# Layer A attention: the preparation of the first output rows held step by step, and 14 gate products moved to the last twelve steps

## The chip, the cores and the metric

The kernel runs on one core of one Trainium2 chip, as a single program. The metric is the device time of one execution in microseconds. A core has five engines with instruction queues of their own: TensorE (PE; its weight loads are PEld), VectorE (DVE), ScalarE (ACT), GpSimd (POOL) and SyncE (SP), which here issues all DMAs. Every queue is worked off in the order in which the program stands; an instruction that waits for a semaphore holds what is queued behind it on its engine.

## The reference, cut to what matters

A decoder of two layers over 2048 positions and 1024 channels, in float32. Only the first layer (A) is touched by the change:

```python
u = rmsnorm(h, norm_a_g[i])
proj = u @ w_in_a[i]
q, k, v, f_logit, gate = jnp.split(proj, [...], axis=-1)
...
o = fox_attention(q, k, v, log_f).reshape(b, s, WIDTH_A)
h = h + (o * jax.nn.silu(gate)) @ w_out_a[i]
```

`fox_attention` is causal softmax attention with 16 heads of 64 channels and a bias from a running sum of forget gates. What matters here are the last two factors: the attention's output `o` is divided by its row sums, multiplied by the SiLU of the gate, and projected with `w_out_a`.

## The kernel before, in words

A float32 product of full precision is made of three products: every operand is split into a high part (rounded to fp32r) and the remainder, and high x high, high x low and low x high are added up in PSUM.

`layer_a` projects q, k, v and the forget logits, runs `attention_a`, and then `out_a`, the output projection. The attention's loop (L1171) has 320 steps: 16 heads, in each four chunks of 512 queries, and for the chunks 2, 4, 6 and 8 steps of two key blocks (20 a head). A step does the following.

- `scores` (L997): up to four products (L1013, L1014) into two `sc` banks; ScalarE takes the exponential into an `st` tile (L1029) and rounds it to `ph` (L1032); **GpSimd subtracts, `pl` = `st` - `ph` (L1033, "the split" below)**; VectorE adds to the row sums (L1042).
- `values` (L1047), three steps later (`V_LAG`): for each key block one product with `ph` and one with `pl` (L1057).
- `ahead`: the maxima of score rows for a later chunk (L968 on TensorE, L976 and L981 on VectorE), whose row is written into the key operand by four small DMAs (L578). These end some steps before the loop does, since no further head follows.
- `feed` (L1155): products of the gate projection (L1099) as filler. There are 768: four chunks of 512 columns, eight row tiles, eight depth tiles, three products each. In step n the filler is brought to (768 - `KEPT`)(n + 1)/320, so 2.25 products a step; `KEPT` = 48 are left for the tail behind the loop. Every 12 products need new gate weights (`wr`, two buffers, 512 KB from DRAM, L1076). Where a chunk of columns begins anew, sixteen operand tiles of 256 KB are loaded as well (L1085). A finished bank of 24 products goes through VectorE and ScalarE (L1110 to L1112) and is stored as `gt` (L1113).

The output projection needs, for each pair of heads and chunk, a prepared operand: main and correction part of the attention's output added, times the reciprocals `rd`, times the gate `gt`, split in high and low (`gated`, L1231: L1240, L1241, L1244, ScalarE's L1245, L1246). The four inputs are loaded by `gated_load` (L1221 to L1226: `om`, `oc`, `gt` and twice `rd`). The first two pairs are prepared inside the attention's loop, on GpSimd: their loads and all five instructions are written in steps 284 and 298 (`PREP_AT`). The third pair's loads are written behind the loop (L1203), and its first add belongs to the projection's first step. The tiles `qn` that take `om` and `gt` have two buffers, so that a pair's loads wait until the pair before has done with them.

The order on an engine is not that of the source: a scheduler takes instructions by their place in the program and by when it believes them ready, and may put a later instruction ahead. `keep_in_program_order` holds an instruction back until those before it in the program have been placed.

Of the kernel before, what the change touches and what calls it, by code (L numbers as in the profile page):

```python
# [13 lines left out]
F32R = mybir.dt.float32r  # L14
# [4 lines left out]
ALU = mybir.AluOpType  # L19
# [4 lines left out]
P = 128  # L24
# [8 lines left out]
CH = 512  # L33
# [10 lines left out]
LOAD_AT = 7  # L44

PREP_AT = (284, 298)

RAW_AT = 302

KEPT = 2 * 3 * NDT  # L50

PAIRS_LOADED = 5
PAIRS_READY = 2
# [47 lines left out]
def f_(ap):  # L101
    return ap.bitcast(F32)


class Pairs:
# [13 lines left out]
    def prepare(self, s, engine=None, pin=False):  # L119
        if s % 4 == 0:  # L120
            self.Y[s // 4] = self.t.sb("big", [P, 4, 2, CH], F32R)
        self.t.gated(self.y(s), self.tiles.pop(s), engine or self.t.nc.vector, pin)
        self.ready = s + 1

    def y(self, s):
        return self.Y[s // 4][:, s % 4]
# [27 lines left out]
class Trunk:  # L154
# [727 lines left out]
    def attention_a(self, op):  # L882


        nc, tc, d = self.nc, self.tc, self.d
# [17 lines left out]
        steps = [(u, p) for u, (h, ch) in enumerate(units) for p in range(2 * ch + 2)]  # L903
# [248 lines left out]
        filler, fed, total = gate(), 0, NCH * NDT * NDT * 3  # L1152
# [18 lines left out]
        for n, (u, p) in enumerate(steps):  # L1171
            h, ch = units[u]
            if n % per_head == LOAD_AT and h + 1 < H:
                more_pieces(len(pieces) + 1)
            target = per * (n + AHEAD + 1) // per_head + 1
            ahead(target - 1)
            ends = len(pending) == V_LAG and closes(pending[0])
            if ends:
                values(pending.pop(0))
            pending.append(scores(n, u, p))  # L1180
            ahead(target)
            if len(pending) > V_LAG and not ends:
                values(pending.pop(0))
            if p == 2 * ch + 1:
                if h == H - 1 and ch in (0, NCH - 1):
                    due.append((n + SUM_LAG, (h, ch and 1, ch + 1)))
                elif ch == NCH - 1 and h == H - 2:
                    due.append((n + SUM_LAG, (h,)))
                elif ch == NCH - 1 and h % 2:
                    due.append((n + SUM_LAG, (h - 1, 0, NCH, 2)))  # L1190
            while due and due[0][0] <= n:
                recips(*due.pop(0)[1])
            if n == 0:
                self.ps("mx", [P, 512])
            feed((total - KEPT) * (n + 1) // len(steps), pause=True)
            if n == RAW_AT:
                raw = self.sb("big", [P, NDT // 2, D])
                for p in range(NDT // 2):
                    op.weight_load(p, raw[:, p])
            if n in PREP_AT:  # L1200
                op.load(PREP_AT.index(n), ("qn", "wh", "qn", "wl"))
                op.prepare(PREP_AT.index(n), nc.gpsimd)
        op.load(2, ("qn", "wh", "qn", "wl"))  # L1203
        gate_bank, weight_slots = "mx", cycle(["st", "wr"])
        for item in pending:
# [11 lines left out]
    def gated_load(self, ch, p, tiles):  # L1217
        nc, d = self.nc, self.d
        rows, cols = slice(p * P, (p + 1) * P), slice(ch * CH, (ch + 1) * CH)
        m, c, g, rb = tiles  # L1220
        nc.sync.dma_start(out=m, in_=d["om"][rows, cols])  # L1221
        nc.sync.dma_start(out=c, in_=d["oc"][rows, cols])
        nc.sync.dma_start(out=g, in_=d["gt"][rows, cols])
        for s in range(2):
            h = 2 * p + s
            nc.sync.dma_start(  # L1226
                out=rb[s * HD : (s + 1) * HD, :],
                in_=d["rd"][h : h + 1, cols].to_broadcast([HD, CH]),
            )

    def gated(self, y, tiles, engine, pin=False):  # L1231

# [455 lines left out]
```

## Time and profile before

| what | us |
|---|---|
| timed runs, median of 3 (lowest, highest) | 2422.66 (2418.39, 2423.58) |
| profiled execution | 2421.78 |
| its span | 2420.0 |
| TensorE busy (share of the span) | 2402.8 (99%) |
| GpSimd busy (share of the span) | 994.6 (41%) |

A row of the timeline gives the start in us, the duration in us, the engine, the source line, the operation and its tiles (out<-in), the shapes, the number of instructions merged, and in brackets the idle time ahead with what ended it. Rows marked SPq are the issue of a DMA, not its transfer. The attention's loop lies between about 596 us (first split) and 1432 us (last split), the tail of gate products ends at 1444 us, and the output projection follows. Numbers behind PE are busy time and, in brackets, the count of instructions. The duration of a TensorE product is modelled and overlaps the next; its pace is read from the distance of starts.

### The profile page before, as it was taken

What the parts mean: (1) busy time and instruction counts of PE and PEld (TensorE: products, weight loads), DVE (VectorE), ACT (ScalarE), POOL (GpSimd) and SP (SyncE); (2) the same over time, 40 slices, a digit from 0 to 9 for tenths busy, and PEclk for the clock granted to TensorE, in tenths of its full rate; (3) what the DMA queues carried; (4) which work ended last, traced back from release to release, by engine and by line L of the source; (5) the groups of instructions that cost most, each with busy time, mean ns of one, the idle gap of its engine ahead of it and who ended that gap; (6) DMA issues with size and microseconds to landing.
All of it is one profiled execution on the core that took longest, in us unless ns stands there. A gap on an engine that the chain in (4) does not pass through costs nothing.

```text
span 2420.0 us, 36279 instructions
## 1 busy us (share of the span) xinstructions
PE 2402.8 (99%) x11960; PEld 2026.4 (84%) x11960; DVE 1732.2 (72%) x4086; ACT 1262.2 (52%) x2504; POOL 994.6 (41%) x642
## 2 busy tenths in 40 slices
PE   9999999999999999999999999999999999999999
PEld 7888899988888888888888888888888888888887
DVE  7656567735898888888888866456766633677775
ACT  5433324323878778877877761135423322466664
POOL 0000000011877777777778862200011000378885
PEclk9999999999999999999999999999999999999999
DMA  6656555677654655566466549975434574765552
GB/s 192 201 170 193 152 154 167 197 229 233 186 165 128 198 165 151 149 207 175 132 178 181 178 134 304 304 248 164 131 92 122 160 253 144 236 213 181 182 183 75
DMA packets 356989, 436.04 MB, mean 180 GB/s; under 512 B 65280, under 2 KB 248608, under 8 KB 350624
## 3 DMA queue, kind: packets, MB, share of 16 engines
q1 hardware_dynamic: 356800, 433.71, 59.3%
q8 instruction: 95, 1.56, 0.3%
q14 instruction: 94, 0.77, 0.1%
HBM read 273.69 MB, written 159.79 MB: 179 GB/s over the span
## 4 chain that ended last, share of the span: by engine, by line
PE 92%; DMA 5%; DVE 1%; ACT 1%; issue 0%; POOL 0%; SPq 0%; ACTq 0%; POOLq 0%; DVEq 0%
PE b L790 31%; PE pa L1057 10%; PE pb L1099 7%; PE pb L1515 7%; PE sc L1013 5%; PE sc L1014 5%; PE mx L968 5%; PE b L1286 4%; PE b L752 4%; PE b L1369 2%; PE pa L1454 2%; PE pb L752 2%; DMA wr<-wg 1%; PE fl L359 1%; PE pa L359 1%; PE pb L359 1%
## 5 line engine op out<-in xcount | busy, mean ns | idle before, releaser
L790 PE MATMUL b<-wh,big 128*128 128x512 f32 (+3 forms) x2560 | 772.2, 374 | 1.1 <-ACT wh L502 0.9
L1033 POOL TENSOR_TENSOR big<-st,big 128x1024 fp32r<-128x1024 f32 (+1 forms) x320 | 656.2, 2071 | 239.2 <-ACT big L1032 158.9
L790 PEld LDWEIGHTS b<-wh,big 128*128 128x128 f32 x2560 | 470.6, 188 | 72.4 <-ACT wh L502 2.8
L790 PE MATMUL b<-wl,big 128*128 128x512 f32 (+3 forms) x1280 | 473.8, 370 | 0.8 <-DVE wl L503 0.7
L1042 DVE TENSOR_TENSOR ac<-ac,st 128x512 f32<-128x512 f32 (+3 forms) x576 | 352.6, 612 | 51.9 <-ACT st L1029 27.2
L1029 ACT ACTIVATE st<-sc 128x512 f32<-128x512 f32 (+1 forms) x512 | 273.6, 583 | 117.5 <-PE sc L1023 48.2
L1057 PE MATMUL pa<-big 128*128 128x512 f32 (+3 forms) x1280 | 318.9, 365 | 0.7 <-POOL big L1033 0.7
L1032 ACT CAST big<-st 128x1024 fp32r<-128x1024 f32 (+1 forms) x320 | 295.3, 923 | 8.5
L790 PEld LDWEIGHTS b<-wl,big 128*128 128x128 f32 x1280 | 241.3, 189 | 37.2 <-DVE wl L503 5.2
L1057 PEld LDWEIGHTS pa<-big 128*128 128x128 f32 x1280 | 229.0, 190 | 39.0 <-POOL big L1033 2.4
L981 DVE TENSOR_REDUCE mt<-mx 128x1 f32<-128x384 f32 (+1 forms) x360 | 214.3, 598 | 30.7 <-PE mx L968 28.2
L1013 PE MATMUL sc<-big 128*128 128x512 f32 (+3 forms) x640 | 232.9, 368 | 0.1
L511 ACT ACTIVATE sq<-b,r 128x512 f32<-128x512 f32 (+2 forms) x128 | 77.8, 608 | 295.4 <-PE b L790 295.4
L1014 PE MATMUL sc<-big 67*128 67x512 f32 (+3 forms) x640 | 229.6, 367 | 0.0
L968 PE MATMUL mx<-big 66*128 66x512 f32 (+2 forms) x600 | 224.9, 380 | 0.2
L1099 PE MATMUL pb<-wh,wr 128*128 128x512 f32 x488 | 177.4, 396 | 5.5 <-DMA wr<-wg 5.3
L513 DVE TENSOR_REDUCE sm<-sq 128x8 f32<-128x512 f32 (+2 forms) x128 | 74.8, 584 | 138.0 <-ACT sq L511 137.8
L892 POOL MEMSET rot<- 128x512 bf16 x1 | 0.5, 525 | 418.3 <-PE pb L359 418.3
L1417 POOL TENSOR_TENSOR big<-big,tri 128x1024 fp32r<-128x1024 f32 x60 | 144.3, 2405 | 59.9 <-DVE big L1414 59.9
L976 DVE CUSTOM_DVE_ANT_0 mx<-mx,rot 128x384 f32<-128x384 f32 (+2 forms) x240 | 146.8, 617 | 17.9 <-PE mx L968 17.3
L1013 PEld LDWEIGHTS sc<-big 128*128 128x128 f32 x640 | 121.7, 190 | 21.7 <-DVE st L560 0.5
L1014 PEld LDWEIGHTS sc<-big 67*128 67x128 f32 x640 | 121.8, 190 | 19.3
(285 smaller groups left out, 4124.0 us busy)
## 6 DMA issues: line engine op xcount, KB each, us to landing
wr<-wg SPq DMA_DIRECT2D x62, 512.0 KB, 4.2
va<-st SPq DMA_DIRECT2D x32, 512.0 KB, 4.7
ka<-st SPq DMA_DIRECT2D x64, 256.0 KB, 3.8
ut<-big SPq DMA_DIRECT2D x16, 1024.0 KB, 7.0
big<-ka SPq DMA_DIRECT2D x16, 1024.0 KB
big<-qa SPq DMA_DIRECT2D x16, 1024.0 KB, 7.8
qb<-st SPq DMA_DIRECT2D x64, 256.0 KB, 3.7
big<-qb SPq DMA_DIRECT2D x16, 1024.0 KB, 7.7
```

The lines of the kernel that those rows point to most:

```text
L790: nc.tensor.matmul(ps[:, :n], u[tb // 4][:, dt, us], W[k][dt], start=(dt == 0 and i == 0), stop=(dt == NDT - 1 and i == 2),)
L968: mm = nc.tensor.matmul(ps, qb[:66, i * P : (i + 1) * P], kb[:66, k0:k1], start=True, stop=True,)
L981: nc.vector.reduce_max(o, ps, axis=AX.X)
L1013: nc.tensor.matmul(o, ka[:, ks], qa[:, qs], start=not (last and n_), stop=False)
L1014: nc.tensor.matmul(o, kb[:, ks], qb[:, qs], start=False, stop=not diag)
L1029: nc.scalar.activation(pf[:, off : off + w], ps[:, :w], AF.Exp, scale=HD**-0.5)
L1032: nc.scalar.copy(ph[:, :tw], pf[:, :tw])
L1033: nc.gpsimd.tensor_tensor(pl[:, :tw], pf[:, :tw], f_(ph[:, :tw]), ALU.subtract)
L1042: nc.vector.tensor_tensor(a_, a_, pf[:, off : off + w], ALU.add)
L1057: nc.tensor.matmul(pv[:, q0 : q0 + w], v[:, k, :], src[:, off : off + w], start=(p == 0 and n_ == 0 and i == 0), stop=(last and n_ == 1 an ...
L1099: nc.tensor.matmul(ps, w[:, dt // 2 % 2, wk, dt % 2, :], us[dt][uk], start=(dt == 0 and i == 0), stop=(dt == NDT - 1 and i == 2),)
L1515: nc.tensor.matmul(ps, yt(i, y, slice(p, p + 1))[:, 0, :], W[nh][p // 4][:, k, p % 4, :], start=(p == 0 and n_ == 0), stop=(p == NDT - 1 a ...
```

## The change

Two things. First, the preparation of the two pairs becomes a generator, `gated_parts`. Its loads are written in steps 284 and 298 as before; the instructions follow from five steps later on (`PREP_LAG`), one a step: the add, two multiplications, a step with nothing, ScalarE's copy, the subtraction. Each is kept in program order. Second, `DENSE` = 14 gate products are taken out of the even spread and added in the last twelve steps (`DENSE_STEPS`): the filler now stands at 706(n + 1)/320, and from step 308 on 14/12 more with every step.

```diff
 PREP_AT = (284, 298)
+PREP_LAG = 5
...
 KEPT = 2 * 3 * NDT
+DENSE = 14
+DENSE_STEPS = 12
...
+    def prepare_parts(self, s):
+        if s % 4 == 0:
+            self.Y[s // 4] = self.t.sb("big", [P, 4, 2, CH], F32R)
+        self.ready = s + 1
+        return self.t.gated_parts(self.y(s), self.tiles.pop(s))
...
-            feed((total - KEPT) * (n + 1) // len(steps), pause=True)
+            ahead_of = DENSE * max(0, n + 1 + DENSE_STEPS - len(steps)) // DENSE_STEPS
+            feed((total - KEPT - DENSE) * (n + 1) // len(steps) + ahead_of, pause=True)
...
             if n in PREP_AT:
-                op.load(PREP_AT.index(n), ("qn", "wh", "qn", "wl"))
-                op.prepare(PREP_AT.index(n), nc.gpsimd)
+                s = PREP_AT.index(n)
+                op.load(s, ("qn", "wh", "qn", "wl"))
+                prepared = op.prepare_parts(s)
+            if any(0 <= n - at - PREP_LAG < 6 for at in PREP_AT):
+                next(prepared, None)
...
+    def gated_parts(self, y, tiles):
+        nc, pin = self.nc, self.tc.keep_in_program_order
+        m, c, g, rb = tiles
+        yh, yl = (y[:, k] for k in range(2))
+        yield pin(nc.gpsimd.tensor_tensor(m, m, c, ALU.add))
+        yield pin(nc.gpsimd.tensor_tensor(m, m, rb, ALU.mult))
+        yield pin(nc.gpsimd.tensor_tensor(m, m, g, ALU.mult))
+        yield
+        yield pin(nc.scalar.copy(yh, m))
+        yield pin(nc.gpsimd.tensor_tensor(yl, m, f_(yh), ALU.subtract))
```

What moves on the engines is seen in the order of the built programs. In the changed kernel the lines of the attention's loop have numbers higher by 9 (the split L1033 is L1042 there, a gate product L1108, a load of `wr` L1085), those of `gated_load` by 13, and those from `gated` on by 24; its pieces of the preparation are L1248, L1249, L1250, ScalarE's L1252, and L1253.

GpSimd, before, from step 273 (head 13) on: `big<-st,big` is a split, `qn<-qn,wh` the first add of a pair, `qn<-qn,wl` and `qn<-qn` its multiplications, `big<-qn,big` its last subtraction. The scheduler has put the preparation eleven steps ahead of the place where it is written.

```order
L1033 TENSOR_TENSOR big<-st,big 128x1024
L1240 TENSOR_TENSOR qn<-qn,wh 128x512
L1241 TENSOR_TENSOR qn<-qn,wl 128x512
L1244 TENSOR_TENSOR qn<-qn 128x512
L1033 TENSOR_TENSOR big<-st,big 128x1024 x3
L1240 TENSOR_TENSOR qn<-qn,wh 128x512
L1033 TENSOR_TENSOR big<-st,big 128x1024
L1241 TENSOR_TENSOR qn<-qn,wl 128x512
```

In the changed program the first pair stands in the second half of head 14, and the second in the last head, with the first add of the third pair (L1264) between; these are the rows from step 302 on:

```order
L1042 TENSOR_TENSOR big<-st,big 128x1024 x2
L1248 TENSOR_TENSOR qn<-qn,wh 128x512
L1042 TENSOR_TENSOR big<-st,big 128x896
L1249 TENSOR_TENSOR qn<-qn,wl 128x512
L1042 TENSOR_TENSOR big<-st,big 128x384
L1250 TENSOR_TENSOR qn<-qn 128x512
L1042 TENSOR_TENSOR big<-st,big 128x1024
L1264 TENSOR_TENSOR qn<-qn,wh 128x512
L1042 TENSOR_TENSOR big<-st,big 128x1024 x2
L1253 TENSOR_TENSOR big<-qn,big 128x512
```

In before only splits stand in the last head's rows on GpSimd. Now five instructions of the preparation stand between its first eight splits, one behind each of several splits.

SyncE, before, ahead of the two gate weights (`wr<-wg`) that step 292 and the next need. `big<-m` is a row of maxima, `om<-sq`, `oc<-sq` and `gt<-sq` are stores of results, and the last two rows are loads for the second and third pair:

```order
L578 DMA big<-m 1x128x1 x8
L1067 DMA om<-sq 64x512
L1113 DMA gt<-sq 128x512
L1068 DMA oc<-sq 64x512
L1076 DMA wr<-wg 128x1024 x2
L1223 DMA qn<-gt 128x512
L1221 DMA qn<-om 128x512
```

The same place in the changed program:

```order
L587 DMA big<-m 1x128x1 x8
L1076 DMA om<-sq 64x512
L1077 DMA oc<-sq 64x512
L1085 DMA wr<-wg 128x1024 x2
L1235 DMA wh<-oc 128x512
L1239 DMA wl<-rd 64x512 x2
L1234 DMA qn<-om 128x512
L587 DMA big<-m 1x128x1 x4
```

The store of a gate tile no longer stands ahead of the two loads of `wr`, and behind them come the second pair's loads, which in before stood some twenty steps earlier.

TensorE, before, from the last products of step 319 with an earlier split (`pa<-big`) on, through its gate products (`pb<-wh,wr`, `pb<-wl,wr`) and the products of the last three splits to the first gate product of the tail (`mx<-wh,st`):

```order
L1057 MATMUL pa<-big 128x512 x4
L1099 MATMUL pb<-wh,wr 128x512
L1099 MATMUL pb<-wl,wr 128x512
L1099 MATMUL pb<-wh,wr 128x512
L1057 MATMUL pa<-big 128x512 x6
L1057 MATMUL pa<-big 128x384 x2
L1057 MATMUL pa<-big 128x256 x2
L1057 MATMUL pa<-big 128x128 x2
L1099 MATMUL mx<-wh,st 128x512
```

The same place in the changed program:

```order
L1066 MATMUL pa<-big 128x512 x4
L1108 MATMUL pb<-wl,wr 128x512
L1108 MATMUL pb<-wh,wr 128x512 x2
L1108 MATMUL pb<-wl,wr 128x512
L1108 MATMUL pb<-wh,wr 128x512
L1066 MATMUL pa<-big 128x512 x6
L1066 MATMUL pa<-big 128x384 x2
L1066 MATMUL pa<-big 128x256 x2
L1066 MATMUL pa<-big 128x128
L1108 MATMUL mx<-wh,st 128x512
```

Three gate products stand in the last step in before, five now, and each of the steps ahead of it has about one more. The tail behind the loop holds 48 in both; the very last product with a split now stands behind 16 of them instead of ahead of all.

## Prediction

> **What bounds the kernel now.** I read the page first, then the windows of 50 us over the whole attention stage, then TensorE's waits, and last the timeline of SyncE, GpSimd and TensorE at the places where a window of TensorE is not full. The page's first part says that TensorE is busy for nearly all of the span:
>
> ```profile
> PE 2402.8 (99%) x11960; PEld 2026.4 (84%) x11960; DVE 1732.2 (72%) x4086; ACT 1262.2 (52%) x2504; POOL 994.6 (41%) x642
> ```
>
> So only what TensorE waits for can be gained, and only what makes it wait can be lost. The waits of the attention's products (L1057, L1099) stand in these rows of the view of waits (whole run: total us, times, longest):
>
> ```profile
> PE pb L1099 <- DMA wr<-wg: 5.3, 5, 1.5
> ...
> PE b L1286 <- DVE big L1297: 0.7, 1, 0.7
> PE pa L1057 <- POOL big L1033: 0.7, 2, 0.4
> ```
>
> The first is a gate product (L1099) that waits for its gate weights `wr`; the last is an output product (L1057) that waits for the low half that GpSimd makes (L1033); the middle one lies in the projection behind the attention. The windows (TensorE's busy time is the first figure behind the length) put the gate waits at the three changes of the gate's chunk, and once more at 1358 us:
>
> ```profile
> 800.00:850.00 50.00, 48.61 (x238) 39.94 (x237) 43.90 (x98) 39.20 (x62) 38.16 (x19) 1.00 0.74 221
> 1000.00:1050.00 50.00, 48.51 (x241) 40.12 (x240) 41.62 (x95) 38.05 (x62) 37.49 (x19) 1.00 0.63 185
> 1200.00:1250.00 50.00, 49.43 (x242) 40.78 (x241) 42.89 (x96) 40.51 (x64) 38.68 (x20) 1.00 0.47 121
> 1250.00:1300.00 50.00, 49.19 (x242) 40.68 (x240) 43.88 (x100) 38.60 (x63) 36.34 (x19) 1.00 0.71 219
> 1300.00:1350.00 50.00, 50.00 (x249) 41.81 (x248) 43.79 (x98) 38.58 (x62) 46.67 (x26) 1.00 0.68 190
> 1350.00:1400.00 50.00, 48.66 (x238) 39.55 (x237) 42.93 (x96) 38.27 (x62) 41.03 (x22) 1.00 0.47 148
> 1400.00:1450.00 50.00, 49.71 (x230) 40.37 (x231) 32.34 (x47) 33.41 (x51) 31.25 (x15) 1.00 0.44 135
> ```
>
> Row by row TensorE lacks 1.39, 1.49, 0.57, 0.81, 0, 1.34 and 0.29 us: 5.9 us, or 0.24% of the span. The window 1300 to 1350 holds most of the old preparation, with GpSimd at 46.67 of 50 us, and TensorE lacks nothing in it. That sets the scale of what can be won. The granted clock is 1.00 in every row.
>
> **The preparation, moved and held.** The view of its tiles gives the first and the last instruction of each preparation on GpSimd, with the shortest, median and longest time in ns and the first and last start:
>
> ```profile
> L1240 POOL TENSOR_TENSOR qn<-qn,wh x3: 1286/1290/1304, 1309.6 to 1366.8; 128x512 f32<-128x512 f32 x3
> ...
> L1246 POOL TENSOR_TENSOR big<-qn,big x2: 1295/1325/1355, 1330.0 to 1363.2; 128x512 fp32r<-128x512 f32 x2
> ```
>
> The work stays the same: four GpSimd instructions of 1.3 us and one ScalarE copy for each of two pairs, and the hoisted first add of a third. The first pair moves to the end of head 14, the second pair and the third's add into the last head, between steps 303 and 309. Taking it away from 1309 to 1368 gains nothing, since TensorE was full there; putting it later is what can cost. There GpSimd works like this in before (steps 302 to 309, then 310 to 319):
>
> ```profile
> 1391.15 4.77 POOL L1033 TENSOR_TENSOR big<-st,big 128x1024 fp32r<-128x1024 f32 x2 [3.17 <-ACT big L1032]
> 1396.19 3.10 POOL L1033 TENSOR_TENSOR big<-st,big 128x896 fp32r<-128x896 f32 x2 [0.27 <-ACT big L1032]
> 1400.73 2.40 POOL L1033 TENSOR_TENSOR big<-st,big 128x1024 fp32r<-128x1024 f32 x1 [1.44 <-ACT big L1032]
> 1403.43 2.41 POOL L1033 TENSOR_TENSOR big<-st,big 128x1024 fp32r<-128x1024 f32 x1 [0.29 <-PE pa L1057]
> 1406.34 7.85 POOL L1033 TENSOR_TENSOR big<-st,big 128x1024 fp32r<-128x1024 f32 x4 [0.51 <-ACT big L1032]
> 1415.02 17.29 POOL L1033 TENSOR_TENSOR big<-st,big 128x1024 fp32r<-128x1024 f32 x8 [0.83 <-ACT big L1032]
> ```
>
> From 1391.15 to 1432.31 that is 41.2 us with 37.8 busy, so 3.4 idle. The second pair and the third's add are five instructions, 6.5 us: 44.3 us of work. GpSimd alone would overrun the old stretch by 3.1 us.
>
> **The 14 products.** One gate product costs what one 128x512 product costs, read from 36 in a row:
>
> ```profile
> 1444.15 8.32 PE L1286 MATMUL b<-big 128*128 128x512 f32 x36
> 1452.31 0.84 PE L1286 MATMUL pa<-big 128*128 128x512 f32 x3
> ```
>
> (1452.31 - 1444.15) / 36 = 0.227 us. Fourteen of them are 3.2 us that leave steps 1 to 308 and come back in steps 309 to 320: nothing in the sum, but the stretch on TensorE grows from 41.2 to 44.4 us, against GpSimd's 44.3. The two edits belong together, and each would be worse alone.
>
> I follow GpSimd's queue by the durations above, counting from step 302 as in before. The old starts give splits 302 to 306 done at 1393.5, 1395.9, 1399.3 (behind the first add), 1401.6 and 1405.3; the third's add ends at 1406.6; splits 307, 308 and 309 end at 1409.0, 1411.4 and 1415.1 (behind the last subtract). TensorE uses a split three steps later:
>
> ```profile
> 1407.76 1.17 PE L1057 MATMUL pa<-big 128*128 128x512 f32 x4
> 1409.23 1.18 PE L1057 MATMUL pa<-big 128*128 128x512 f32 x4
> ```
>
> These are the products of steps 307 and 308. With the extra products ahead of them they start near 1408.7 and 1410.3, and the low half is their second product. So TensorE would wait about 0.3 and then 0.9 us. Just ahead of this the order gives TensorE seven gate products in one piece, held back from the two steps before; if they come late against GpSimd's queue they cover the wait, if not, nothing does. **I take +0.6 us**, half of 1.2, with the ends 0 and +3 (the whole overrun of 3.1 us). From step 310 on a full step takes TensorE 8 + 3.4 products, 2.59 us, against 2.40 on GpSimd, which catches up by 0.19 us a step. In before it was 10.25 products, 2.32 us, and GpSimd set the pace: that is the 0.7 us of L1057. **I take -0.7 us** for it, ends -0.7 and 0.
>
> **SyncE's queue.** The loads for the preparation are issued there, in order, between the loads of gate weights. In before the queue stands for them (the view of SyncE's waits, 1300 to 1445 us):
>
> ```profile
> SPq L1067 <- ACT sq L1065: 20.8, 7, 7.5
> ...
> SPq L1221 <- DMA qn<-gt: 5.6, 1, 5.6
> ...
> SPq L1222 <- DMA wh<-oc: 3.6, 1, 3.6
> ```
>
> In after it stands in new places: the second pair's loads behind the first's multiplications (their tiles are reused), the third's behind the second's, and the rows of the maxima, the stores and the next `wr` queue up behind them. The late load of 1358 us in before looks like this, on SyncE and on the weight loader:
>
> ```profile
> 1351.53 0.55 SPq L1067 DMA_DIRECT2D om<-sq  x1
> 1352.17 0.54 SPq L1113 DMA_DIRECT2D gt<-sq  x1
> 1352.76 0.47 SPq L1068 DMA_DIRECT2D oc<-sq  x1
> 1353.32 1.04 SPq L1076 DMA_DIRECT2D wr<-wg  x2
> ...
> 1358.60 0.19 PEld L1099 LDWEIGHTS pb<-wh,wr 128*128 128x128 f32 x1 [1.78 <-DMA wr<-wg]
> ```
>
> Nobody blocks the queue here; it is full, and the load lands 5.3 us after its issue, when TensorE has been idle for 1.34 us. In after the same load stands behind one issue less (the gate store L1113 has moved), 0.54 us earlier, so this wait falls to about 0.8 us: **-0.5 us**. The preparation does not remove it, and the three chunk changes keep their sixteen operand loads in the same queue. Yet with 14 products fewer by step 308 every change of weights falls up to six steps later, among other neighbours in the queue. Five loads of sixty were late, by 1.06 us on the mean; if as many are late by chance, the number varies by its root, 2.2, and the sum by 2.4 us either way.
>
> The Trainium skill ("SBUF — State Buffer", section "The DMA setup-cost knee") puts a transfer at 2 us plus its bytes at 436 GB/s, so 3.2 us for these 512 KB. By that the load issued at 1353.32 would have landed at 1356.5, before TensorE asked for it, there would have been no wait to shorten, and my sum would lose its -0.5 us. The trace speaks against it, with 5.3 us here and this row for all loads of `wr`:
>
> ```profile
> DMA to landing us min/median/max: 3.7/4.2/6.4
> ```
>
> **The sum.** +0.6 - 0.7 - 0.5 = -0.6 us against the profiled execution's 2421.78 us (span 2420.0 and 1.78 around it): 2421.2. That execution lies 0.9 us below the median of the three timed runs (2418.39, 2422.66 and 2423.58), from which the same sum gives 2422.1. I predict 2421.6, between the two. The three runs differ by 5.2 us; about 0.2%, 4.8 us, is what a measurement of this kernel can tell from no change.
>
> **Rivals.**
> First, slower: GpSimd stands in the last head. Its third add needs the load of `om` (L1221), which SyncE issues behind the store of reciprocals (L947), at 1396.63 in before; two issues later and 4.2 us to landing make 1401.7, and the add comes at 1405.3, a margin of 3.6 us. If SyncE is held longer than that, the add blocks the splits behind it. SyncE's longest wait in this stretch is the 7.5 us quoted above (a store that waits for the copy of an output); this is the row of the store of reciprocals:
>
> ```profile
> 1396.63 0.45 SPq L947 DMA_DIRECT2D rd<-sq  x1
> ```
>
> With that, GpSimd stands 7.5 - 3.6 = 3.9 us more, on top of the overrun's 3.1 without cover, and TensorE waits up to 7 us less what the gate products hide (seven, 1.6 us): +5.4 us, 2427.2. Against it: the blocked issue must fall into one of a few steps. 5%.
>
> Second, clearly faster: the late loads of weights come in time as well, because SyncE no longer interleaves loads of three pairs. -5.3 (all gate waits), -0.7 (GpSimd's) and, if the projection's first loads also start earlier, -0.7: 2421.78 - 6.7 = 2415.1. For it: two of the five places lie near the old loads. Against it: three belong to chunk changes that the edit does not touch. 9%.
>
> Third, nothing: the instructions are held where the order says, but the overrun on GpSimd (+1.2 uncovered) eats what the late load and the tail give back (-1.2): 2421.8. 28%.
>
> My forecast takes the remaining 58%. It and the third lie within 0.2%: 0.86 for the same, against 0.09 for faster and 0.05 for slower. **The range** takes the 2.4 us of the late loads and half the spread of the three runs, 2.6 us, together as squares, 3.5 us either way, which also holds GpSimd's +3; below, the 0.7 us of the projection comes on top: 2417.4 to 2425.1.
>
> **What would show it.** Right, if in the changed profile: TensorE's waits for `wr` are again four to six with three at the chunk changes; the wait at step 292 is under 1.34 us; GpSimd runs without idle time from about step 303 to 312, five of its instructions of 1.3 us among the splits; L1057 waits for GpSimd at step 307 or 308 for under 1 us, and no longer at the end. Wrong, if GpSimd idles in the last head on a landing DMA with TensorE idle behind it, or if the gate waits fall below 2 us in all.

## The result and the profile after

The change made the kernel slower. Five runs of the changed kernel have a median of 2429.17 us (2426.73 to 2431.19), five of the kernel before, on the same chip, 2419.14; the ratio is 1.0039, 95% interval 1.0029 to 1.0050. In a later job it was 2430.76 against 2418.46, ratio 1.0050 (1.0038 to 1.0063). So it lost 10 to 12 us, and the forecast of 2421.6 (2417.4 to 2425.1) was wrong.

TensorE is busy for 2.9 us longer than before, on a span that is 7.5 us longer; this is the page's first part for the changed kernel (span 2427.5 us):

```profile
PE 2405.7 (99%) x11960; PEld 2030.0 (84%) x11960; DVE 1730.5 (71%) x4086; ACT 1262.1 (52%) x2504; POOL 993.6 (41%) x642
```

The view of TensorE's waits (us in total, times, longest) now begins so:

```profile
PE pb L1108 <- DMA wr<-wg: 8.1, 6, 2.3
PE sc L1022 <- ACT st L1038: 3.7, 2, 3.4
...
PE pa L1066 <- POOL big L1042: 0.5, 2, 0.4
```

The gate's waits have grown from 5.3 to 8.1 us, and a wait that before does not have stands second: scores (L1022) that wait until ScalarE (L1038) has freed their bank. GpSimd's split, to which the forecast gave the only loss, is waited for 0.5 us in all. The same windows as before show where this lies (the figure behind the five engines is the granted clock):

```profile
1000.00:1050.00 50.00, 47.86 (x233) 40.03 (x232) 40.13 (x92) 36.24 (x59) 35.72 (x18) 0.97 0.61 180
...
1250.00:1300.00 50.00, 47.58 (x225) 38.84 (x223) 40.52 (x90) 36.54 (x59) 35.60 (x18) 0.97 0.71 220
...
1400.00:1450.00 50.00, 46.39 (x205) 36.84 (x204) 29.01 (x46) 34.56 (x53) 37.03 (x20) 0.93 0.46 143
```

TensorE lacks 2.14, 2.42 and 3.61 us in them, where it lacked 1.49, 0.81 and 0.29; and in the same three rows the granted clock is no longer 1.00. The waits explain only part of the loss; the rest is slow products behind them. TensorE's timeline where the gate's second chunk ends shows it:

```profile
1043.45 0.59 PE L1108 MATMUL pb<-wh,wr 128*128 128x512 f32 x1 [2.02 <-DMA wr<-wg]
1043.84 0.63 PE L1108 MATMUL pb<-wl,wr 128*128 128x512 f32 x1
1044.27 1.06 PE L1108 MATMUL pb<-wh,wr 128*128 128x512 f32 x2
1045.12 0.63 PE L1108 MATMUL pb<-wl,wr 128*128 128x512 f32 x1
```

Behind the wait of 2.02 us, two products take 1045.12 - 1044.27 = 0.85 us, 0.425 us each, where 0.227 is the pace. The granted clock is 0.50 there, for one stretch of 3.41 us:

```profile
1040.31:1043.72 3.41, 1.39 (x8) 1.14 (x7) 2.99 (x6) 1.87 (x3) 3.22 (x2) 1.00 0.73 257
1043.72:1047.14 3.42, 3.42 (x9) 2.68 (x9) 0.03 (x1) 0.00 (x0) 0.94 (x1) 0.50 0.35 101
```

In before the same product waited for 1.49 us, and the pace behind it was full at once:

```profile
1029.78 0.50 PE L1099 MATMUL pb<-wh,wr 128*128 128x512 f32 x1 [1.49 <-DMA wr<-wg]
...
1030.34 0.62 PE L1099 MATMUL pb<-wh,wr 128*128 128x512 f32 x2
1030.80 0.39 PE L1099 MATMUL pb<-wl,wr 128*128 128x512 f32 x1
```

The largest loss is in the last head. Four engines tell it. On SyncE a load of `om` (L1234) for the third pair is issued at 1404.36, 5.2 us after the end of the issue ahead of it, and the store of a gate tile (L1122) stands two issues behind it:

```profile
1398.80 0.33 SPq L1235 DMA_DIRECT2D wh<-oc  x1
1404.36 0.33 SPq L1234 DMA_DIRECT2D qn<-om  x1
1404.74 1.02 SPq L1239 DMA_DIRECT2D wl<-rd  x1
1405.85 0.54 SPq L1122 DMA_DIRECT2D gt<-sq  x1
```

On GpSimd the second pair's last multiplication (L1250) reads a `qn` tile whose buffer this load takes, and it ends at 1403.02 + 1.31 = 1404.33. So SyncE stood for a tile that GpSimd still read (the view of SyncE's waits gives 5.2 us for L1250). GpSimd itself then waits 1.32 us for that load:

```profile
1403.02 1.31 POOL L1250 TENSOR_TENSOR qn<-qn 128x512 f32<-128x512 f32 x1
1404.28 2.40 POOL L1042 TENSOR_TENSOR big<-st,big 128x1024 fp32r<-128x1024 f32 x1
1408.00 1.26 POOL L1264 TENSOR_TENSOR qn<-qn,wh 128x512 f32<-128x512 f32 x1 [1.32 <-DMA qn<-om]
```

On ScalarE the copy of an attention output into `sq` (L1074) needs one of two `sq` buffers, and waits 4.20 us for the gate store to have read its own; the exponentials are queued behind it:

```profile
1409.19 0.58 ACT L1074 COPY sq<-pa 128x512 f32<-128x512 f32 x1 [4.20 <-DMA gt<-sq]
1409.67 1.09 ACT L1038 ACTIVATE st<-sc 128x512 f32<-128x512 f32 x2
```

And TensorE, with all banks for scores full, waits 3.43 us and then runs at half pace: the four products from 1411.35 take until 1413.05 (not 1412.26), and the half pace lasts until about 1415.8, two of the stretches of 3.41 us.

```profile
1410.33 0.80 PE L1022 MATMUL sc<-big 128*128 128x512 f32 x1 [3.43 <-ACT st L1038]
1410.92 0.63 PE L1023 MATMUL sc<-big 67*128 67x512 f32 x1
1411.35 1.91 PE L1066 MATMUL pa<-big 128*128 128x512 f32 x4
1413.05 0.63 PE L1108 MATMUL pb<-wl,wr 128*128 128x512 f32 x1
...
1415.91 1.17 PE L1066 MATMUL pa<-big 128*128 128x512 f32 x4
```

Added up over both traces, from the distance of TensorE's starts over the usual one: the last head cost 5.4 us more than before, the changes of the chunk near 1042 and 1267 us 2.2 and 2.3 us more, smaller places 1.4 us together, and the attention as a whole took 11.3 us longer (916.1 against 904.8, first to last product). It began 0.8 us earlier, and behind it the projection is 1.4 us shorter and the rest 1.6 us, which leaves the 7.5 us between the two profiled spans.

### The profile page after: what moved, and what is told of

Read it like the earlier page. It is cut to its first block, busy times and chain, and to the rows that moved or that the text cites. A ratio compares the mean times of both kernels' runs of the same rounds, so it can differ in the third digit from the quotient of the medians.

```text
span 2427.5 us, 36272 instructions
## 1 busy us (share of the span) xinstructions
PE 2405.7 (99%) x11960; PEld 2030.0 (84%) x11960; DVE 1730.5 (71%) x4086; ACT 1262.1 (52%) x2504; POOL 993.6 (41%) x642
## 5 line engine op out<-in xcount | busy, mean ns | idle before, releaser
L1042 POOL TENSOR_TENSOR big<-st,big 128x1024 fp32r<-128x1024 f32 (+1 forms) x320 | 656.0, 2069 | 250.9 <-ACT big L1041 152.5
L1038 ACT ACTIVATE st<-sc 128x512 f32<-128x512 f32 (+1 forms) x512 | 273.1, 582 | 113.0 <-PE sc L1032 54.5
L1022 PE MATMUL sc<-big 128*128 128x512 f32 (+3 forms) x640 | 234.5, 370 | 3.8 <-ACT st L1038 3.7
L1108 PE MATMUL pb<-wh,wr 128*128 128x512 f32 x488 | 172.8, 399 | 8.1 <-DMA wr<-wg 8.1
L1022 PEld LDWEIGHTS sc<-big 128*128 128x128 f32 x640 | 122.3, 191 | 27.1 <-ACT st L1038 5.6
```

The source lines that it names most:

```text
L1022: nc.tensor.matmul(o, ka[:, ks], qa[:, qs], start=not (last and n_), stop=False)
L1038: nc.scalar.activation(pf[:, off : off + w], ps[:, :w], AF.Exp, scale=HD**-0.5)
L1042: nc.gpsimd.tensor_tensor(pl[:, :tw], pf[:, :tw], f_(ph[:, :tw]), ALU.subtract)
L1108: nc.tensor.matmul(ps, w[:, dt // 2 % 2, wk, dt % 2, :], us[dt][uk], start=(dt == 0 and i == 0), stop=(dt == NDT - 1 and i == 2),)
```

## The experiments

Theory Q: three things add up. The 14 products move the changes of the gate's chunk to steps at which the weights arrive later; the third pair's load holds SyncE in the last head, with a store behind it for which ScalarE waits; and a wait of TensorE above some 2 us halves its clock for a while. Rival G: it is GpSimd's work in the last head. Rival N: which loads are late is chance. Theory T came later: the gate's waits are in the order of two loads. Times are medians, each against the runs of before in the same job (2418.4 to 2419.7 in four jobs).

**The hold alone** (e1_hold): the changed kernel with

```diff
-DENSE = 14
+DENSE = 0
```

> The changed kernel with DENSE = 0: the preparation is held step by step, and no gate product is moved. Theory Q (the store of a gate tile is stuck on SyncE behind the load of om for the third pair, so ScalarE stands, TensorE waits 3.4 us, and then runs 11 products at half pace): without the 14 products the gate tile is finished five steps earlier and its store stands ahead of that load in the order, so TensorE has no wait over 2 us between 1390 and 1430 us, the gate waits are those of before (5.3 us), and the median is within 3 us of before, 2417 to 2422. Rival G (GpSimd overruns the last head): the same five instructions now stand against 3.2 us fewer of TensorE's products, so the waits for the split grow: TensorE waits 3 us or more for L1042, and the time is that of the changed kernel or above, 2429 to 2432. Rival N (only chance decides which loads are late): any place, 2417 to 2431, with no pattern at the last head.

Measured: 2422.67 against 2418.55, ratio 1.0023 (1.0012 to 1.0033): slower by 4 us, which Q did not expect. The last head's waits (1395 to 1440 us), and GpSimd's timeline there:

```profile
PE pa L1066 <- POOL big L1042: 2.5, 3, 1.8
```

```profile
1404.61 1.30 POOL L1264 TENSOR_TENSOR qn<-qn,wh 128x512 f32<-128x512 f32 x1 [1.30 <-PE sc L1023]
1405.86 4.70 POOL L1042 TENSOR_TENSOR big<-st,big 128x1024 fp32r<-128x1024 f32 x2
```

Here the gate store is out of the way, as Q said (the stores are issued at 1380.24 and 1412.24), and TensorE does not wait for ScalarE. But the third pair's add stands idle for 1.30 us (the engine named had long been done; the load of `om` had been issued at 1400.97 and was landing) and works for 1.30, and the splits behind it come late. G has part of the truth when the 14 products are not there.

**The 14 products alone** (e2_dense): the kernel before with only the two lines of `feed` from the change.

> The kernel before with only the 14 gate products moved to the last twelve steps; the preparation stays where it was. Theory Q: nothing stands in the last head (no wait over 2 us from 1390 to 1430 us), but the stream of gate products up to step 308 is that of the changed kernel, so the weights at the changes of the chunk arrive as late as there (waits of about 1.6, 2.3 and 2.6 us near 805, 1042 and 1267 us), with half pace behind the two longer ones: 4 to 6 us over before, 2422 to 2426. Rival G: no preparation in the last head, so no loss at all, 2417 to 2421. Rival N: the late loads fall anew, 2417 to 2426, at other places than in the changed kernel.

Measured: 2424.49 against 2418.55, ratio 1.0023 (1.0014 to 1.0032). As Q said, and against G: nothing stands in the last head, and yet 3.4 to 7.7 us are lost. Its waits and windows:

```profile
PE pb L1101 <- DMA wr<-wg: 7.5, 6, 2.8
```

```profile
1000.00:1050.00 50.00, 47.06 (x231) 39.36 (x230) 39.52 (x91) 35.54 (x58) 35.82 (x18) 0.97 0.60 174
1250.00:1300.00 50.00, 47.94 (x226) 39.13 (x225) 40.91 (x91) 37.05 (x59) 36.07 (x18) 0.97 0.70 218
1400.00:1450.00 50.00, 49.82 (x233) 40.25 (x232) 30.86 (x51) 34.94 (x53) 32.19 (x16) 1.00 0.45 139
```

The places are those of the changed kernel, with the same drop of the clock to 0.97; the last row is as full as in before. Counted from 0, the gate products 372 and 564 wait here, each the first that needs the weights of a chunk's last twelve. The same two wait, for 1.5 to 3.9 us, in all five profiles in which the 14 products are taken out evenly (the changed kernel's two, e2_dense, e3_third, e10_third_308), which chance (N) does not explain.

**The third pair's loads held behind the loop** (e3_third): the changed kernel, with each of the five loads of `gated_load` for that pair held in program order:

```diff
-        op.load(2, ("qn", "wh", "qn", "wl"))
+        op.load(2, ("qn", "wh", "qn", "wl"), pin=True)
```

> The changed kernel with only the five loads of the third pair held in program order, so that SyncE issues them behind the loop; the third's first add follows them out of the last head. Theory Q: the gate store is no longer behind the load of om, ScalarE does not stand, and the wait of 3.4 us and the half pace behind it (together 5.6 to 6 us) are gone: 2422 to 2425, unless the third pair is then late for the projection (a wait behind 1449 us, up to 3 us). Rival G: one of five GpSimd instructions leaves the stretch, at most 1.3 us are gained: 2427 to 2429. Rival N: 2424 to 2431, the wait in the last head stays or moves.

Measured: 2427.05, ratio 1.0032 (1.0019 to 1.0045). The mechanism is as Q said: from 1395 to 1435 us TensorE now is full at full clock (second row), where the changed kernel (first row) lacks 3.43 us and 29 products:

```profile
1395.00:1435.00 40.00, 36.57 (x161) 28.88 (x160) 23.02 (x42) 29.64 (x48) 35.14 (x20) 0.91 0.39 114
```

```profile
1395.00:1435.00 40.00, 40.00 (x190) 32.09 (x189) 27.73 (x50) 35.00 (x55) 37.41 (x21) 1.00 0.33 102
```

The time is not as expected: it is 2 us above Q's range and lies in the one that G gave, so that here only the trace speaks for Q. Its profile has a wait of 3.9 us at the second change of the chunk, with half pace behind it, where the first profile of the changed kernel had 2.0: these waits differ from one execution to the next.

**Half pace by itself** (e4_clock). It leaves out the whole computation: bursts of 36 products, with gaps of sixteen lengths.

```diff
+            for i in range(BURST):
+                nc.tensor.matmul(ps, w, u, start=True, stop=True)
+            nc.vector.tensor_single_scalar(tmp, ps[:, :P], 0.09, ALU.mult)
+            for i in range(k):
+                nc.vector.tensor_single_scalar(tmp, tmp, 1.0, ALU.mult)
```

> Not the reference's computation: bursts of 36 products of 128x512 on TensorE, and between them a chain of 3 to 18 VectorE operations on 128x128 that TensorE waits for, 16 lengths in 5 rounds; nothing else runs and no DMA moves. Theory Q: the half pace comes from the wait itself. Behind gaps under about 2 us products start 0.227 us apart at once; behind longer ones they start about 0.42 us apart for some 4 us, 9 to 11 products, whatever else the chip does; the length from which it begins shows in the sixteen lengths. Rival: the half pace comes from the traffic at those places (loads of 512 KB, 300 GB/s), and here every product starts 0.227 us behind the one before, at every length.

Measured, two bursts on TensorE's timeline (a burst's start, its length, and in brackets the gap ahead of it):

```profile
622.17 9.86 PE L127 MATMUL ps<-u,w 128*128 128x512 f32 x36 [2.83 <-DVE w L133]
...
821.16 8.40 PE L127 MATMUL ps<-u,w 128*128 128x512 f32 x36 [2.83 <-DVE w L133]
```

Nothing else runs here, and a burst behind a long gap takes about 10.0 us, not 8.4: as a rule some eight products at half pace, 1.6 us. It is the gap, then, and not traffic. Over all 80 bursts (the lengths in turn, five rounds) half pace followed none of the gaps up to 1.78 us, 1 of 5 at 2.05, none of 5 at 2.31, 4 of 5 at 2.57, 2 of 5 at 2.83, 4 of 5 at 3.09, and every one from 3.35 on; in seven bursts it lasted for 12 to 14 products.

The two bursts above have the same gap, and only the first is slow. What tells them apart is where the gap lies. In each trace all changes of the granted clock lie on one grid with steps of 3.41 us. The rows are steps of that grid, the first two about the first gap, the others about the second (ScalarE does nothing here and has no column):

```profile
618.41:621.82 3.41, 0.93 (x5) 0.43 (x3) 2.13 (x10) 0.00 (x0) 1.00 0.00 0
621.82:625.24 3.42, 3.07 (x7) 2.48 (x8) 0.20 (x1) 0.00 (x0) 0.50 0.00 0
816.38:819.79 3.41, 1.95 (x9) 1.29 (x7) 1.25 (x6) 0.00 (x0) 1.00 0.00 0
819.79:823.21 3.42, 2.05 (x9) 1.76 (x10) 1.08 (x5) 0.00 (x0) 1.00 0.01 2
```

The first gap puts 2.48 us of idle time into one step, and the clock of the next step is 0.50; the second is split, 1.46 and 1.37 us, and the clock stays at 1.00. Over the whole test each of the 45 steps at full clock with 1.90 us or more of idle time was followed by a step at half, and none with 1.85 or less. Behind a step at half clock with 0.69 us or more of idle time came another one, behind one with 0.55 or less the full clock: so the half clock lasted one step or two.

The same grid sorts the waits of the attention. In all its traces every step with 1.77 us or more of idle time was followed by half clock, and of those with less only one was, of 1.47 us (e16_hold), while others of up to 1.53 us were not. The waits of 1.99 us in e5_late and 1.73 in the changed kernel, which look long enough, fall into two steps each, with at most 1.22 us in one. Why the bound lies a little lower here than in the bursts stays open. The Trainium skill ("TensorE: Matmul & The Clock Gate", section "Part 1: The HAM clock gate (the "warmup" mystery)") says that an idle window of about 3.4 us brings TensorE down to half its clock until it has been busy for about as long. The half pace, 0.425 against 0.227 us, and the steps of 3.41 us agree with that; that a whole window has to be idle does not, since 1.90 us in one were enough here.

**The 14 products taken later** (e5_late), and **with the third pair's loads held as well** (e6_late_third):

```diff
-            feed((total - KEPT - DENSE) * (n + 1) // len(steps) + ahead_of, pause=True)
+            taken = DENSE * min(max(0, n + 1 - 260), 48) // 48
+            feed((total - KEPT) * (n + 1) // len(steps) - taken + ahead_of, pause=True)
```

> The changed kernel, but the 14 products are taken from steps 260 to 307 only, so that the three changes of the gate's chunk fall on the steps of before, while the filler from step 308 on is the changed kernel's. Theory Q: the waits at the chunk changes are those of before (up to 1.7 us, no half pace behind them), worth 4 to 6 us, while the stand of ScalarE in the last head stays (a wait of over 3 us near 1400, half pace behind it): 4 to 6 us over before, 2422 to 2425. Rival N (late loads fall by chance): as the changed kernel, 2426 to 2430, or anything between.

> As e5_late, and the third pair's loads are held in program order behind the loop as in e3_third. Theory Q: the last head has no wait over 1 us either, and both costs of the change are gone: within 2 us of before, 2417 to 2421, and 4 to 6 us under e5_late of the same job. Rival G (GpSimd's overrun is the cost in the last head): no more than 1.3 us under e5_late.

Measured: e5_late 2420.36 against 2418.42, ratio 1.0009 (1.0000 to 1.0017); e6_late_third 2418.52, ratio 0.9999 (0.9990 to 1.0007). With the chunks' changes back on their old steps the gate's waits are back at 5.0 us, with no half pace behind them, and 8 to 10 us of the loss are gone (a part of them in the last head, see below); with the third pair's loads behind the loop as well nothing of it is left. Between the two lie 1.8 us, where Q had 4 to 6 and G at most 1.3; with runs spread over 7 to 8 us each this pair alone does not decide between them. In e5_late's profile the wait of the last head is there, but shorter, and the clock holds.

```profile
PE pb L1108 <- DMA wr<-wg: 5.0, 5, 1.5
PE sc L1022 <- ACT st L1038: 2.0, 1, 2.0
```

ScalarE's view of waits there (1385 to 1420 us) names another store behind the same load, that of the reciprocals:

```profile
ACT sq L1074 <- DMA rd<-sq: 2.4, 1, 2.4
```

**Weights asked for in another order** (e7_ahead), an edit to the kernel before. At the end of a chunk the code asks for the next chunk's first weights before those of its own last twelve products; the two take turns with two buffers, so that the weights of the last twelve get the buffer that is read until the product just ahead of them. (In before the gate products 180, 372 and 564, counted from 0, wait: each is the first of a chunk's last twelve.)

```diff
-                            w = gate_weights(ft, dt) if ft or dt else first
+                            if turn and dt:
+                                w = second
+                            else:
+                                w = gate_weights(ft, dt) if ft or dt else first
+                            if turn and not dt:
+                                second = gate_weights(ft, NDT // 2)
```

> The kernel before with one edit: where a chunk of the gate ends, the weights for its last twelve products are asked for before those of the next chunk, so that they take the buffer that is free and not the one that has just been read. Theory T (the wait at each chunk change is the landing of a load that cannot be issued before the product just ahead of it): the three waits of 1.3, 1.6 and 1.0 us near 801, 1028 and 1258 us are gone, 2414 to 2416 against 2418.5. Rival (the queue or the traffic makes the load late, not its buffer): the waits stay, 2417 to 2420.

Measured: 2414.93 against 2418.42, ratio 0.9988 (0.9979 to 0.9997). Theory T holds: no wait is left at the chunk's changes, and one late load near 1355 us remains (1.8 us, with half pace behind it in the profiled execution, which with 2418.86 us is one of the longer ones):

```profile
PE pb L1104 <- DMA wr<-wg: 1.8, 1, 1.8
```

```profile
1000.00:1050.00 50.00, 50.00 (x248) 41.34 (x247) 43.30 (x98) 39.63 (x64) 38.25 (x20) 1.00 0.64 195
1250.00:1300.00 50.00, 50.00 (x248) 41.51 (x247) 44.87 (x99) 41.48 (x67) 38.03 (x19) 1.00 0.72 216
1350.00:1400.00 50.00, 48.22 (x229) 39.25 (x228) 40.41 (x89) 36.35 (x59) 40.09 (x22) 0.97 0.45 142
```

**The changed kernel with both mends** (e8_ahead_third: e3_third and e7_ahead together):

> The changed kernel with both mends: the weights asked for in the order of e7_ahead, and the third pair's loads held behind the loop as in e3_third. Theories Q and T: no wait for wr at a chunk change and no stand in the last head; what is left of the change is below 1.5 us either way, so 2413 to 2417, level with e7_ahead of the same job. Rival G or N: 3 us or more over e7_ahead.

Measured: 2416.22, ratio 0.9985 (0.9976 to 0.9994): level with e7_ahead.

**The hold alone, third pair behind the loop** (e9_hold_third: `DENSE = 0` in e3_third), and **the third pair loaded in step 308** (e10_third_308 with the 14 products, e13_hold_308 without): in the last two the pinned load stands in the loop.

```diff
+            if n == THIRD_AT:
+                op.load(2, ("qn", "wh", "qn", "wl"), pin=True)
```

> The preparation held step by step, no gate products moved (as e1_hold), and the third pair's loads held behind the loop. In e1_hold TensorE waited 1.8 and 0.3 us for GpSimd's splits near 1408 and 1410 us, and ran at half pace behind the first. Theory Q (GpSimd came late there because the third pair's add waited for its load, 1.30 us, and took 1.30 us itself): the waits for L1042 fall below 1 us in all and the time is that of before, 2417 to 2420, 2 to 5 us under e1_hold's 2422.7. Rival G (the four instructions of the second pair are too many by themselves for a head without the moved products): TensorE still waits over 1.5 us there, 2420 to 2423.

> The changed kernel, but the third pair's loads are written in step 308 and held in program order: SyncE issues the waiting gate store ahead of them, while GpSimd still has all five instructions in the last head (the third's add now near step 311). Theory Q (SyncE's order is the cost, not GpSimd's work): TensorE has no wait over 1 us from 1395 to 1430 us; the changes of the chunk stay as in the changed kernel, so 2422 to 2426, as e3_third or a little below. Rival G: five instructions in the last head still cost 3 us or more there, 2426 to 2431.

> The held preparation without the 14 products, with the third pair's loads written in step 308. If the loss of e9_hold_third is the third pair coming late for the projection, the waits of 2 us behind the loop (1446 to 1484 us) are gone, and without a wait in the last head the time is that of before, 2417.5 to 2420.5. If the loss is GpSimd's work in a head without the moved products, its fifth instruction is back and TensorE waits 1.5 to 3 us for L1043: 2421 to 2425.

Measured: e9_hold_third 2425.18 against 2418.46, ratio 1.0028 (1.0018 to 1.0038), 5 to 8 us above what Q expected; e10_third_308 2426.71, ratio 1.0035 (1.0023 to 1.0048); e13_hold_308 2420.45 against 2419.69, ratio 1.0004 (0.9995 to 1.0013).

In e10_third_308 GpSimd has all its work in the last head and no idle time at all, and TensorE lacks 0.48 us:

```profile
1395.00:1435.00 40.00, 39.52 (x187) 31.60 (x187) 25.91 (x45) 34.50 (x54) 40.00 (x21) 1.00 0.47 139
```

By its time e10_third_308 lies 0.7 us above Q's range and inside G's. But it is 4.0 us under the changed kernel of the same job (2430.76), only the third pair's loads have moved, and GpSimd still has its five instructions there. That ends rival G for the changed kernel: its cost in the last head was SyncE's order. (The chunks' changes are still late in it, 7.1 us of waits for `wr`, with half clock behind two of them.) In e13_hold_308, without the 14 products, TensorE still waits 1.7 us for splits in the last head, but no step of the clock's grid has enough of it, and the clock holds. In e9_hold_third TensorE's wait for splits in the last head went from 2.5 to 1.0 us, but the projection behind the loop now waits for VectorE: its split of the output weights (L149) stands behind the preparation of pairs whose loads land late, and the wait of 0.8 us is for the one that starts at 1471.63 (1467.58 in e13_hold_308):

```profile
PE b L1311 <- DVE big L149: 1.0, 2, 0.8
```

Its profiled execution lacks 1.2 us of TensorE from 1440 to 1490 us, where e13_hold_308 lacks nothing:

```profile
1440.00:1490.00 50.00, 48.78 (x210) 38.63 (x209) 26.60 (x35) 9.56 (x14) 12.13 (x9) 1.00 0.94 298
```

So without the 14 products the third pair is best loaded inside the loop, but behind the store; with them, loads behind the loop cost nothing that was seen (e6_late_third). What its profiles show does not add up to the whole 6.7 us of e9_hold_third; the rest stays open.

**Second profiles** of the changed kernel (e11_again, also timed: 2430.76), of before (e14_before, 2419.88), of e9_hold_third (e15_again, 2422.56) and of e1_hold (e16_hold, 2422.19):

> The changed kernel again, beside the others of this job. Theory Q: 2426 to 2431; a second profile shows the wait of ScalarE's copy for the store of the gate tile in the last head (over 2 us of TensorE's time) and waits of 2 to 4 us for wr near 1042 and 1267 us, with half pace behind each wait of over 2 us. Rival N: the places differ from the first profile, the last head among them.

> The kernel before once more, for a second profile. Theory T: the gate waits stand at the same three changes of the chunk near 801, 1028 and 1258 us again, each between 0.8 and 2 us, since they follow from the order; what makes single executions differ by some us lies in other loads (1246 and 1357 us) and behind the attention.

> e9_hold_third once more, for a second profile. If the third pair's late loads are the cost, TensorE waits again in the projection between 1444 and 1490 us, 2 us or more in all; in the last head it waits under 1.5 us.

> e1_hold once more, for a second profile. Theory Q: the wait for GpSimd's split behind the third's add near 1408 us comes again (1.5 to 3 us), with or without half pace behind it as it is over or under 2 us.

The changed kernel's second profile has the same places, larger waits at the changes of the chunk, and half clock at one place more, behind the wait near 1360 us (1.87):

```profile
PE pb L1108 <- DMA wr<-wg: 9.1, 6, 3.4
PE sc L1022 <- ACT st L1038: 3.5, 2, 3.3
```

e1_hold's wait for the split came again (1.9 us, half pace behind it), and so did e9_hold_third's for VectorE (1.0 us of the 2 or more expected). Before's second profile has 4.3 us of gate waits, again in five places, but those near 1028 and 1259 us are only 0.2 and 0.5 us, less than the 0.8 that T expected: the places come from the order, their size differs between executions.

**All mended** (e12_all: e6_late_third with the weights in e7_ahead's order):

> e6_late_third with the weights asked for as in e7_ahead: the change with all three costs mended, so that it differs from e7_ahead only in the held preparation, the 14 products (taken from steps 260 to 307) and the later loads of the third pair. Theory Q: with the costs gone nothing of the change is left that TensorE waits for; level with e7_ahead, 2413 to 2416. If the change has a gain of its own that the costs covered up, 2411 to 2413.

Measured: 2415.09 against 2418.46, ratio 0.9987 (0.9978 to 0.9996). Level with e7_ahead (0.9988, in another job): the held preparation and the 14 products have, with their costs mended, no gain of their own that these runs can tell. The version that beats both kernels is the mend of the weights' order, alone or with them, by about 3.4 us.

## Why the prediction was wrong, point by point

- **What bounds the kernel**: right. TensorE is full but for its waits, and what makes it wait can be lost. But the prediction priced a wait at its length. One that puts about 1.8 us into a single step of the clock's grid also halves the clock of the next, some eight products and up to 1.7 us more (1.7 again where a second step follows), and before's longest, 1.49 us in one step, lay just under that. So a small delay of these loads could cost double.
- **The baseline**: the profiled execution (2421.78) and the three runs stood high. Over five jobs before's median lies between 2418.4 and 2419.7, so 2421.6 began 2 to 3 us too high, and the real miss is larger than the two numbers show.
- **"Fourteen of them are 3.2 us that leave steps 1 to 308 and come back in steps 309 to 320: nothing in the sum"**: this step failed first. The products themselves cost nothing, but taking them out evenly from step 1 moves each change of the gate's chunk by two to five steps: e2_dense lost 5.9 us by this alone, and e5_late, which takes them behind the last change, got it back. The prediction saw that every change of weights would fall later and called it chance, 2.4 us either way. Three of its five late loads stood at the chunks' changes, where the order makes them late (e7_ahead); that was a pattern and not chance. Why a load lands later on the new steps (near 1035.73 us two loads of weights stand directly one behind the other, and the median landing of all loads of `wr` is 5.2 us against 4.2) was not tried apart and stays open.
- **SyncE's queue in the last head**: this failed next. The prediction said that the third pair's loads would stand behind the second's multiplications and that the stores would queue up behind them, and gave this no term in its sum: it priced what would delay the load of `om`, and not what that load would hold up. Its rival had the place (the last head), the resource (SyncE) and nearly the price (+5.4 us; 5.4 measured), with a chance of 5%, but another path: the load waits for GpSimd to free its tile, the gate store behind it is late, and so ScalarE's copy, the exponentials, and TensorE. The prediction's own sign of error, GpSimd idle on a landing load with TensorE idle behind it, was met by half: GpSimd stood for 1.32 us, but TensorE's idle time stood behind ScalarE.
- **"The two edits belong together, and each would be worse alone"**: each alone lost 4 to 6 us, and both together 10 to 12. The products did cover GpSimd's work, as argued (waits for splits in the last head of 0.8 us in e10_third_308, 1.7 in e13_hold_308 without them), but they also finish the gate tile some steps later, and its store falls right behind the blocked load. In e1_hold that store was out of the way.
- **+0.6 for GpSimd's overrun**: of the right size where SyncE is not in the way: 0.48 us lacking in e10_third_308. (By the prediction's own times the first of its two waits is nearer 0.1 than 0.3 us, since the low half is the second product.) **-0.7 in the tail**: the row was misread. Of the two waits in it one, 0.36 us, stands at 598.23, where the attention begins, and is still there in the changed kernel (0.37); only the other, 0.29 us at 1431.39, could be won, and 0.18 us of waiting is left at the loop's end. **-0.5 for the late load at 1358**: that load (for gate product 648, counted from 0) is late no more, but the one before it (636) is, and TensorE waits 1.73 us for it near 1359, where it was 1.34.
- **The price of a load**: the estimate of 3.2 us for 512 KB by the Trainium skill's 2 us plus bytes at 436 GB/s ("SBUF — State Buffer", section "The DMA setup-cost knee") was rejected rightly; in the changed kernel no load of `wr` lands that fast.

```profile
DMA to landing us min/median/max: 3.9/5.2/7.3
```

## What to carry to other kernels

When an instruction is moved, look not only at what it waits for but at what is queued behind it on that engine, and who waits for that, one engine further: here a load held a store, the store a buffer, the buffer ScalarE, and ScalarE the exponentials that TensorE needs. Taking filler out of an even spread moves every event that the filler's count triggers, loads above all, so take it from a place behind the last of them. A wait that comes at the same event three times is no chance: look at which buffer the late load is given. And a wait of TensorE that is long enough to halve its clock has to be priced with the slow products behind it.

## What the runs showed of the hardware

The granted clock of TensorE changed only on a grid with steps of 3.41 us, to 0.50 and back to 1.00, and at 0.50 a product of 128x512 took 0.425 us instead of 0.227. A step at full clock was followed by one at half if TensorE was idle in it for 1.90 us or more in the bursts (never up to 1.85), and for 1.77 us or more in the attention (up to 1.53 us it was not, but for one step of 1.47). So the same wait can cost nothing more than its length when it falls into two steps, and up to 1.7 us more for each step at half clock when it falls into one; gaps up to 1.78 us were never followed by it in the bursts, and gaps from 3.35 us on always. A kernel whose waits lie just below the bound can lose more to a small delay than the delay.
